# A two-layer attention trunk on one core: exponentials that stay in PSUM, a top-k search by sums of signs, and a new table of segments

## The chip, the cores and the metric

The kernel runs on one core of one Trainium2 chip. The metric is device time in microseconds for one execution of the program. The core has five instruction streams that run side by side and wait for each other through semaphores: TensorE (matmuls and transposes, which write to PSUM; PE in the profile, its weight loads PEld), VectorE (DVE), ScalarE (ACT), GpSimd (POOL) and SyncE (SP), which issues the DMAs. PSUM has eight banks of 512 float32 columns for each of 128 partitions.

## The reference

One sequence of 1024 tokens, 1024 wide, passes two residual layers in float32.

```python
for layer in range(DEPTH):                       # 2
    h = rms_norm(x, ln_g[layer])
    u = h @ w_in                                 # one combined projection
    if layer % 2 == 0:                           # even: A latent attention, B native sparse attention
        y1 = mla_mixer(...) * silu(a_gate)
        y2 = nsa_mixer(...) * silu(b_gate)
    else:                                        # odd: C selected sparse attention, D mLSTM
        y1 = dsa_mixer(...) * silu(c_gate)
        y2 = mlstm_mixer(...) * silu(d_gate)
    y_m = mem_xattn(m_q, mem, ...)
    mix = concatenate([y1, y2, y_m * silu(m_gate)])
    x = x + mix @ w_out[layer]
```

Two pieces matter here. Every attention computes scores, a softmax over them and a product with the values. And the selected sparse attention of the odd layer lets each token attend only to the 256 earlier tokens that an index score ranks highest:

```python
score = einsum('bqh,bqhs->bqs', iw, relu(einsum('bqhd,bsd->bqhs', iq, ik)))
score = where(kpos <= t, score, NEG)
_, sel = lax.top_k(score, 256)
```

## The kernel before

**Who sets the order.** The program is not issued as it is written. Each operation is recorded (class Recorder, line 160) with a cost and with what it depends on; a list scheduler (order, line 302) then places the operations on the five engines and picks the engine where an operation may run on several (flex, line 176: copies go to ACT or DVE, sums and differences to DVE or POOL). Priority comes from the table SEG (line 680): each named piece of work has a start and an end, on which its operations are spread. Tiles come from slots: 8 PSUM banks, 30 pages of 4 KB and 32 of 2 KB in SBUF, and small ones (LIMITS, line 639). Every instruction carries the same source line in the profile, so the profile is read by names of tiles. Five streams result, each in a fixed order: an instruction that waits holds up all behind it on its engine.

**Precision.** Matmuls take fp16. A float32 operand is split in two fp16 halves, hi and lo, and a product takes three matmuls. So each weight and each activation costs a cast (hi) and a subtraction (lo).

**Attention** (attention, line 1277) runs over units of up to 512 columns of scores, or one head where a head has more: for each tile of 128 queries, four heads. One unit passes these steps:

- u_S (1162): matmuls write the scores to PSUM (one bank, or two over 512 columns). DVE takes the negated maximum of each row (nm). In the selected attention, DVE first adds the mask (dmask) and writes the sum to an SBUF page, smask, taking the maximum in the same instruction. Then 11 ln 2 is added to the offset (nm<-nm,lnp, on DVE or POOL), so that the exponentials come out scaled by 2048.
- u_exp (1215): ACT writes exp(score + nm) to an SBUF page P, with the row sums.
- u_split (1224): a part of the units, the turned ones (TURN, line 701: half in latent and native attention, three quarters in selected attention, all in memory attention), are split here: PS is P in two fp16 halves, a cast on ACT or DVE and a subtraction on DVE or POOL.
- u_T (1234): a turned unit is transposed by a DMA, PT<-PS. The other units are transposed by TensorE into PSUM, and ACT copies the high half out (PT); u_lo (1251) subtracts for the low half on DVE.
- u_PV (1257): the product with the values.

With the sizes of this program, 160 units are turned: 104 in the even layer, 56 in the odd one (16 of memory attention, 40 of selected attention, 24 of these 40 with 640 columns or more).

**The top-k search** (topk, line 2049) runs once for query tiles 2 to 4 and once for 5 to 7, on scores of 384 to 1024 columns. It finds the 256th largest score of each row bit by bit: one round for the sign and 31 for the other bits. In each round and for each tile, DVE compares the scores with a candidate and writes ones and zeros (tkj<-score, or tkj<-stop, where stop is the upper half of the scores as bf16, which is enough for the first 15 bits), and ACT sums them (tkj<-tkj, into tkc). Three tiny DVE instructions then set the next candidate (tka, tkd, tkb). After the search DVE builds the mask from comparisons with the threshold and a running count (tkg, tke, tkp, dmask). The search is spread among the projections of the odd layer and the mLSTM.

**v_scale** (line 1107) chooses a power of two for each value tensor and gives its inverse for the result.

Of the kernel before, what the change touches and what calls it, by code (L numbers as in the profile page):

```python
# [8 lines left out]
F = mybir.dt.float32  # L9
R = mybir.dt.float32r  # L10
BF = mybir.dt.bfloat16
H = mybir.dt.float16
I32 = mybir.dt.int32
# [6 lines left out]
NBYTES = {F: 4, R: 4, BF: 2, H: 2, I32: 4}  # L20
# [616 lines left out]
LNP = float(np.float32(11 * np.log(2.0)))  # L637
# [24 lines left out]
def shape_constants():  # L662
# [8 lines left out]
    for i in range(NT):  # L671
# [8 lines left out]
SEG = dict(setup=(-540.765888, -490.733443), norm=(12.964708, 132.050679), e_agate=(31.455813, 704.234339), kv0=(167.224773,  # L680
           345.119047), late=(175.636113, 461.177491), nsak=(275.848244, 1055.795764), q1=(476.701035, 603.438676),
           cmp=(484.672636, 639.334256), nsav=(624.336051, 851.116142), e_kv1=(652.6, 653.6), e_lat=(663.1, 841.289575),
           e_bgate=(688.806149, 749.106149), q0=(713.750502, 956.450502), kv1=(725, 935.4), e_bq=(743.2, 988.9), e_mq=(762.470888,
           932.2), e_kv2=(794.4, 841.5), nsa=(850.7, 1310.2), tab1=(897.605545, 1585.900938), mla0=(911.5, 1001.5), mla1=(952.8,
           1035.2), mem1=(1004.344435, 1330.229828), oA0=(1007.9, 1178.4), mkv0=(1037.7, 1137.062), mem0=(1060.581418, 1262.6),
           oBM0=(1118.8, 1360.2), o_idx=(1297.169979, 1412.178903), topk0=(1312.341201, 1905.3), o_og1=(1334.12618, 1624.221757),
           o_cgate=(1379.576354, 1777.449577), topk1=(1430.809671, 1885.899198), o_og0=(1492.923662, 1808.788497),
           o_mq=(1651.070557, 1759.482667), o_cq=(1677.868104, 1840.650339), o_dqk=(1707.761464, 1804.647378), mlstm=(1753.080505,
           2015.6), o_dv=(1790.7, 1900.9), mkv1=(1795.03316, 1858.78446), oBM1=(1913.5, 2201.9), cv=(1942.975868, 2132.206114),
           dsa=(1984.716978, 2256.916978), oA1=(2154.023358, 2441.25515))  # L690


LOENG = "GV"
# [10 lines left out]
class Trunk:  # L704
# [88 lines left out]
    def setup(self):  # L793
# [9 lines left out]
        self.lnp = self.const([128, 4], F, "lnp")  # L803
        V.memset(self.lnp, LNP)
# [302 lines left out]
    def v_scale(self, views, nh, c=1):  # L1107
# [12 lines left out]
        V.tensor_scalar(e[:, 0, 0:nh], self.spread(m, nh), 1e-30, None, op0=OP.max)  # L1120
        V.tensor_scalar(e[:, 0, 0:nh].bitcast(I32), e[:, 0, 0:nh].bitcast(I32), 0x7F800000, None, op0=OP.bitwise_and)
        V.tensor_scalar(e[:, 1, 0:nh].bitcast(I32), e[:, 0, 0:nh].bitcast(I32), -1.0, float(268 << 23), op0=OP.mult, op1=OP.add)
        V.tensor_scalar(e[:, 2, 0:nh].bitcast(I32), e[:, 0, 0:nh].bitcast(I32), float((14 + c) << 23), None, op0=OP.subtract)
# [38 lines left out]
    def u_S(self, u):  # L1162
# [43 lines left out]
        self.tt(nm, nm, self.lnp[:, 0:per], OP.add, NMENG)  # L1206
# [8 lines left out]
    def u_exp(self, u):  # L1215
        g = u["grp"]
        n, st = u["n"], u["st"]
        p = u["p"] = self.page("P", [128, n * len(u["heads"])])
        for j, h in enumerate(u["heads"]):
            src = self.like(u["sm"][:, j * n:(j + 1) * n], n) if "sm" in u else self.head(u, j)  # L1220
            self.S.activation(self.like(p[:, j * n:(j + 1) * n], n), src, AF.Exp, bias=u["nm"][:, j:j + 1], scale=1.0,
                              accum_out=g["rs"][:, h:h + 1])

    def u_split(self, u):

        if not u["turn"]:
            return
        n = u["n"] * len(u["heads"])
        ps = u["ps"] = self.page("PS", [128, 2, n], H)
        p = u["p"][:, 0:n]  # L1230
        self.copy(ps[:, 0], p)
        self.tt(ps[:, 1], p, ps[:, 0], OP.subtract, LOENG)

    def u_T(self, u):
# [8 lines left out]
        for b0 in range(0, nb, 4):  # L1243
# [4 lines left out]
            self.S.activation(pt[:, 0, b0:b1].rearrange("p k c -> p (k c)"), t[:, 0:128 * (b1 - b0)], AF.Copy)  # L1248
            u["tt"].append((b0, b1, t))

    def u_lo(self, u):
        pt = u["pt"]
        for b0, b1, t in u.get("tt", []):
            f = lambda x: pt[:, x, b0:b1].rearrange("p k c -> p (k c)")
            self.V.tensor_tensor(out=f(1), in0=t[:, 0:128 * (b1 - b0)], in1=f(0), op=OP.subtract)
# [719 lines left out]
    def odd(self, hT, x1tail=None):  # L1975
# [73 lines left out]
        def topk(tiles):  # L2049


            scs = [scores(i, qf) for i, qf in tiles]
            m = len(tiles)
            tops = []
# [4 lines left out]
            cand, base, acc = (self.tiny(m, I32, x) for x in ("tkd", "tkb", "tka"))  # L2059
# [6 lines left out]
            count(0.0, scs)  # L2066
            V.tensor_scalar(base, cnt, 255.5, -1.0, op0=OP.is_lt, op1=OP.mult)
# [398 lines left out]
```

## Time and profile before

| | us |
|---|---|
| median of 3 runs | 1545.11 (1543.31 to 1551.86) |
| the profiled execution | 1550.77 |
| its span, first to last instruction | 1548.9 |
| TensorE busy | 1392.3 |
| DVE busy | 1378.1 |
| ACT busy | 1048.5 |
| POOL busy | 419.7 |
| mean granted TensorE clock | 0.956 |

Busy time is the time in which an engine had at least one instruction running. Rows of groups read: line, engine, operation, output tile <- input tiles, shape and count | busy us, mean ns of one | idle us of the engine before them, and what ended it. A granted clock of 1.00 is full speed.

### The profile page before, as it was taken

To read this page: it belongs to the slowest core of one execution; us is meant where nothing else is said; L and a number is where in the kernel's file an instruction comes from. 1 tells how busy PE (TensorE), PEld (TensorE's weight loads), DVE (VectorE), ACT (ScalarE), POOL (GpSimd) and SP (SyncE) were. 2 spreads that over 40 slices of the span, in tenths; PEclk is the share of its full clock that TensorE was granted. 3 is DMA by queue.
4 is the path that set the end of the run, shared out by engine and by line. 5 is a ranking of instruction groups with operands and counts; after the bars stand their busy time and mean duration, and the time that the engine had idled before them with its cause. 6 is when DMAs were issued, how large, how long until landed. Compare 5 with 4: busy or idle time off the path is not lost.

```text
span 1548.9 us, 30286 instructions
## 1 busy us (share of the span) xinstructions
PE 1392.3 (90%) x10407; PEld 797.4 (51%) x10407; DVE 1378.1 (89%) x3813; ACT 1048.5 (68%) x2498; POOL 419.7 (27%) x527
## 2 busy tenths in 40 slices
PE   4999999978888778969889999999989879998988
PEld 1445546545556655546555554444444455656544
DVE  7765989999999988899889999999999989798994
ACT  7633775576767777786686689999875763466650
POOL 1311244546633242243323200003330212121220
PEclk9999999989999999989999999999998867699999
DMA  9826522367496798979997413201431285299995
GB/s 289 195 75 172 158 71 93 88 150 159 100 179 114 156 183 236 220 138 205 209 235 174 108 48 131 81 25 51 123 109 51 62 181 133 74 207 235 212 232 162
DMA packets 441850, 225.49 MB, mean 146 GB/s; under 512 B 378080, under 2 KB 404320, under 8 KB 441696
## 3 DMA queue, kind: packets, MB, share of 16 engines
q1 hardware_dynamic: 441696, 223.57, 61.0%
q8 instruction: 81, 1.33, 0.4%
q14 instruction: 73, 0.60, 0.1%
HBM read 83.61 MB, written 46.66 MB: 84 GB/s over the span
## 4 chain that ended last, share of the span: by engine, by line
PE 31%; DVE 13%; DMA 4%; issue 2%; ACT 1%; POOL 0%; SPq 0%; ACTq 0%; DVEq 0%
PE psum L558 31%; DMA PT<-PS 3%; DVE tkj L558 1%; DVE nm L558 1%; DVE smask L558 1%; DVE PS L558 1%; DVE wl L558 1%; DVE tkp L558 1%; DVE osp L558 1%; DVE row L558 1%; DVE tke L558 0%; DVE PT L558 0%; DMA oT<-osp 0%; DMA gate<-gate_d 0%; DVE x L558 0%
## 5 line engine op out<-in xcount | busy, mean ns | idle before, releaser
L558 PE MATMUL psum<-wl,hT 128*128 128x512 f16 (+3 forms) x2880 | 669.0, 374 | 11.2 <-DMA hT<-nh 4.0
L558 PEld LDWEIGHTS <-hT 128*128 128x128 f16 x2880 | 280.2, 99 | 315.9 <-issue 36.4
L558 PE MATMUL psum<-wl,oT 128*128 128x512 f16 x960 | 266.3, 382 | 5.7 <-DVE mixM L558 1.9
L558 PEld LDWEIGHTS <-PT 128*128 128x128 f16 x3792 | 223.7, 102 | 92.0 <-DMA PT<-PS 50.7
L558 ACT ACTIVATE P<-psum,nm 128x256 f32<-128x256 f32 (+8 forms) x336 | 191.8, 582 | 90.9 <-POOL nm L558 37.2
L558 POOL TENSOR_TENSOR ms<-ms,nhalf 128x4 f32<-128x4 f32 (+3 forms) x105 | 114.2, 1097 | 430.6 <-DVE ms L558 261.4
L558 PE MATMUL psum<-nv,PT 128*128 128x64 f16 x1584 | 174.8, 195 | 19.6 <-DMA PT<-PS 16.7
L558 DVE TENSOR_REDUCE nm<-psum 128x2 f32<-128x512 f32 (+8 forms) x216 | 162.9, 764 | 16.7 <-PE psum L558 16.4
L558 ACT ACTIVATE tkj<-tkj 128x512 bf16<-128x512 bf16 (+5 forms) x192 | 149.9, 783 | 17.2 <-DVE tkj L558 13.0
L558 PEld LDWEIGHTS <-oT 128*128 128x128 f16 x960 | 93.2, 99 | 102.5 <-issue 6.9
L558 DVE TENSOR_TENSOR PS<-P,PS 128x512 f16<-128x512 f32 (+6 forms) x138 | 116.8, 849 | 1.3 <-ACT PS L558 1.2
L558 PE MATMUL psum<-cst,P 128*128 128x128 f32 x502 | 102.8, 292 | 13.2 <-ACT P L558 9.1
L558 PEld LDWEIGHTS <-qf 128*128 128x128 f16 x832 | 77.6, 103 | 49.3 <-issue 15.2
L558 ACT ACTIVATE wj<-wr 128x1024 bf16<-128x1024 f32 (+4 forms) x76 | 77.7, 1024 | 27.8 <-DMA wr<-w_out 16.7
L558 ACT ACTIVATE PT<-psum 128x512 f16<-128x512 f32 (+3 forms) x160 | 76.5, 504 | 29.3 <-PE psum L558 21.7
L558 PE MATMUL psum<-nkst,qf 128*128 128x320 f16 (+5 forms) x384 | 90.2, 319 | 5.8 <-DVE PT L558 2.5
L558 DVE TENSOR_TENSOR wl<-wr,wl 128x1024 f16<-128x1024 f32 (+3 forms) x79 | 93.7, 1190 | 1.8 <-ACT wl L558 1.6
L558 DVE TENSOR_TENSOR PT<-psum,PT 128x512 f16<-128x512 f32 (+3 forms) x160 | 88.1, 566 | 2.0 <-ACT PT L558 1.7
L558 PE MATMUL psum<-cvp,PT 128*128 128x64 f16 x864 | 70.9, 195 | 13.1 <-DMA PT<-PS 10.1
L558 PEld LDWEIGHTS psum<-cst,P 128*128 128x128 f32 x502 | 65.7, 142 | 32.0 <-ACT P L558 13.6
L558 PE MATMUL psum<-vp,PT 128*128 128x64 f16 x864 | 65.3, 197 | 11.9 <-DMA PT<-PS 6.7
L558 POOL TENSOR_TENSOR nm<-nm,lnp 128x1 f32<-128x1 f32 (+2 forms) x116 | 30.6, 265 | 149.1 <-DVE nm L558 133.2
(494 smaller groups left out, 2894.0 us busy)
## 6 DMA issues: line engine op xcount, KB each, us to landing
wr<-even_w_in SPq DMA_DIRECT2D x20, 512.0 KB, 6.0
wr<-w_out SPq DMA_DIRECT2D x20, 512.0 KB, 5.1
wr<-odd_w_in SPq DMA_DIRECT2D x20, 512.0 KB, 4.9
gate<-gate_d SPq DMA_DIRECT2D x32, 256.0 KB, 3.8
gate_d<-gu SPq DMA_DIRECT2D x24, 256.0 KB, 2.2
qa_d<-mqT SPq DMA_DIRECT2D x16, 384.0 KB, 2.4
xt<-x SPq DMA_DIRECT2D x8, 512.0 KB, 10.3
x<-x SPq DMA_DIRECT2D x8, 512.0 KB, 4.7
```

The costliest lines, as they stand in the source:

```text
L558: r = getattr(engines[o.eng], meth)(*[res(a) for a in args], **{k: res(v) for k, v in kw.items()})
```

## The change

It has three parts and a new table.

1. **The split.** The offset 11 ln 2 goes; exponentials are no longer scaled. In a turned unit ACT writes the exponential over the scores, in PSUM. The cast multiplies by 2048, and the subtraction is one DVE instruction that computes 2048 x - hi (sub with a scale, line 769: scalar_tensor_tensor, on DVE only). The masked scores of the selected attention also stay in PSUM. Units that aren't turned still write P to SBUF; their factor of 2048 moves to the copy out of the transpose's PSUM tile. v_scale's inverse has 11 more in its exponent, since the row sums have lost the 2048.

2. **The search.** In each round ACT computes the sign of (threshold - score), or with the other sign, and sums it; one DVE instruction compares the sum with a limit. For the lower 16 bits the scores are replaced once, for each tile, by a page tkr: the lower half of a score where its upper half equals the threshold found, a large number where it is above, zero where it is below. No comparison on DVE is left in the rounds.

3. **The table** SEG has other numbers.

```diff
-SEG = dict(setup=(-540.765888, -490.733443), norm=(12.964708, 132.050679), e_agate=(31.455813, 704.234339), kv0=(167.224773,
...
+SEG = dict(setup=(-1576.69593, -601.132494), mem1=(-688.598351, 20.410205), e_agate=(30.600801, 726.724683), norm=(40.663363,
...
     def u_S(self, u):
...
         if g.get("addmask") is not None:
-            sm = u["sm"] = self.page("smask")
             for j in range(per):
-                V.tensor_tensor_reduce(out=self.like(sm[:, j * n:(j + 1) * n], n), in0=self.head(u, j),
-                                       in1=self.like(g["addmask"], n), scale=1.0,
+                V.tensor_tensor_reduce(out=self.head(u, j), in0=self.head(u, j), in1=self.like(g["addmask"], n), scale=1.0,
                                        scalar=-3e38, op0=OP.add, op1=OP.max, accum_out=nm[:, j:j + 1])
-            V.tensor_scalar(nm, nm, -1.0, LNP, op0=OP.mult, op1=OP.add)
-            return
+            V.tensor_scalar(nm, nm, -1.0, None, op0=OP.mult)
...
-        self.tt(nm, nm, self.lnp[:, 0:per], OP.add, NMENG)
...
     def u_exp(self, u):
         g = u["grp"]
-        n, st = u["n"], u["st"]
-        p = u["p"] = self.page("P", [128, n * len(u["heads"])])
+        n = u["n"]
+        if not u["turn"]:
+            u["p"] = self.page("P", [128, n * len(u["heads"])])
         for j, h in enumerate(u["heads"]):
-            src = self.like(u["sm"][:, j * n:(j + 1) * n], n) if "sm" in u else self.head(u, j)
-            self.S.activation(self.like(p[:, j * n:(j + 1) * n], n), src, AF.Exp, bias=u["nm"][:, j:j + 1], scale=1.0,
-                              accum_out=g["rs"][:, h:h + 1])
+            src = self.head(u, j)
+            dst = src if u["turn"] else self.like(u["p"][:, j * n:(j + 1) * n], n)
+            self.S.activation(dst, src, AF.Exp, bias=u["nm"][:, j:j + 1], scale=1.0, accum_out=g["rs"][:, h:h + 1])
     def u_split(self, u):
...
-        p = u["p"][:, 0:n]
-        self.copy(ps[:, 0], p)
-        self.tt(ps[:, 1], p, ps[:, 0], OP.subtract, LOENG)
+        self.copy(f(0), src, scale=PSCALE)
+        self.sub(f(1), src, f(0), scale=PSCALE)
...
         def topk(tiles):
...
-            def count(thr, data):
-                for j, sc in enumerate(data):
-                    junk = self.page("tkj", sc.shape, BF)
-                    V.tensor_scalar(junk, sc, thr if isinstance(thr, float) else thr[:, j:j + 1], None, op0=OP.is_ge)
-                    S.activation(junk, junk, AF.Copy, accum_out=cnt[:, j:j + 1])
...
-            for bit in range(30, -1, -1):
-                count(cand.bitcast(F), tops if bit >= 16 else scs)
-                V.tensor_scalar(acc, cnt, 255.5, float(1 << bit), op0=OP.is_gt, op1=OP.mult)
-                if bit:
-                    V.scalar_tensor_tensor(out=cand, in0=acc, scalar=1 << (bit - 1), in1=base, op0=OP.bitwise_xor, op1=OP.bitwise_xor)
-                V.tensor_tensor(out=base, in0=base, in1=acc, op=OP.bitwise_xor)
...
+            def search(data, bits, up, level, side):
+                V.tensor_scalar(nxt, base, up(bits[0]), None, op0=OP.bitwise_xor)
+                for x, bit in enumerate(bits):
+                    t = level(nxt if x == 0 else thr)
+                    for j, d in enumerate(data):
+                        junk = self.page("tkj", d.shape, BF)
+                        S.activation(junk, d, AF.Sign, bias=t[:, j:j + 1], scale=side if side == -1.0 else side[:, j:j + 1], accum_out=cnt[:, j:j + 1])
+                    if x + 1 < len(bits):
+                        V.tensor_scalar(nxt, base, up(bits[x + 1]), None, op0=OP.bitwise_xor)
+                    V.scalar_tensor_tensor(out=acc, in0=cnt, scalar=1.0, in1=lim, op0=OP.mult, op1=OP.is_lt)
+                    if x + 1 < len(bits):
+                        V.scalar_tensor_tensor(out=thr, in0=acc, scalar=bit, in1=nxt, op0=OP.logical_shift_left, op1=OP.bitwise_xor)
+                    V.scalar_tensor_tensor(out=base, in0=acc, scalar=bit, in1=base, op0=OP.logical_shift_left, op1=OP.bitwise_xor)
...
+            search(tops, list(range(30, 15, -1)), lambda b: (1 << b) - (1 << 15), lambda t: t.bitcast(F), isg)
...
+                V.tensor_scalar(eq, tops[j], c(sig), c(top), op0=OP.mult, op1=OP.is_equal)
+                V.tensor_scalar(ab, tops[j], c(sig), c(top), op0=OP.mult, op1=OP.is_gt)
+                r = self.page("tkr", sc.shape)
+                V.scalar_tensor_tensor(out=r, in0=sc.bitcast(U16)[:, 0::2], scalar=1.0, in1=eq, op0=OP.add, op1=OP.mult)
+                V.scalar_tensor_tensor(out=r, in0=ab, scalar=131072.0, in1=r, op0=OP.mult, op1=OP.add)
...
+            search(low, list(range(15, -1, -1)), lambda b: 1 << b, half, -1.0)
```

**In the streams: DVE, lower bits of the search, before.** tkj is the comparison of a tile's scores, tkd the candidate, tka and tkb the round's result; 384, 512 and 640 columns belong to the first search, 768, 896 and 1024 to the second. wl and wr are weights, the rest belongs to the projections.

```order
L558 SCALAR_TENSOR_TENSOR tkd_13821<-tka_13879,tkb_13815 128x3
L558 SCALAR_TENSOR_TENSOR gu_14738<-gth_14761,gu_14738 128x256
L558 TENSOR_TENSOR tkb_13815<-tkb_13815,tka_13879 128x3
L558 CAST wl_14802<-wr_13902 128x1024
L558 TENSOR_SCALAR tkj_14808<-score_13222,tkd_13821 128x768
L558 TENSOR_SCALAR tkj_14815<-score_12765,tkd_13430 128x512
L558 TENSOR_TENSOR wl_14802<-wr_13902,wl_14802 128x1024
L558 TENSOR_SCALAR tkj_14829<-score_13350,tkd_13821 128x896
```

The same engine after, also in the lower bits: tkn is the next candidate before the round's result, tkv the threshold plus a half; row belongs to the mLSTM.

```order
L559 SCALAR_TENSOR_TENSOR tka_13605<-tkc_13098,tkl_102 128x3
L559 COPY mp_112<-row_3335_15341 4x7
L559 TENSOR_TENSOR qsq_15058<-qu_15056,tab_11926 128x512
L559 SCALAR_TENSOR_TENSOR tkd_13608<-tka_13605,tkn_114 128x3
L559 SCALAR_TENSOR_TENSOR tkb_110<-tka_13605,tkb_110 128x3
L559 SCALAR_TENSOR_TENSOR ogu_15309<-ogt_15287,ogu_15309 128x256
L559 TENSOR_SCALAR tkv_14590<-tkd_13608 128x3
```

The wide comparisons have left DVE's stream; four or five instructions on three columns stand in their place in each round.

**ACT, selected attention at 896 columns, before.** P is the exponential, rs its row sums, PS its high half, PT a transposed unit's.

```order
L558 ACTIVATE P_19144,rs_19129<-smask_19109,nm_19110 128x896
L558 ACTIVATE PT_19164<-psum 128x384
L558 ACTIVATE PT_19164<-psum 128x512
L558 ACTIVATE P_19180,rs_19129<-smask_19148,nm_19149 128x896
L558 ACTIVATE osp_19206<-mixA_18488,oe_19160 128x512
L558 ACTIVATE PS_19210<-P_19180 128x896
```

After, at the same size:

```order
L559 ACTIVATE P_18695,rs_18696<-psum,nm_18671 128x896
L559 ACTIVATE psum,rs_18696<-psum,nm_18680 128x2x448
L559 ACTIVATE psum,rs_18696<-psum,nm_18703 128x2x448
L559 ACTIVATE PT_18738<-psum 128x512
L559 ACTIVATE PT_18738<-psum 128x384
L559 ACTIVATE PS_18751<-psum 128x896
```

The exponential of a turned unit goes back to its two PSUM banks and the high half is read from there; in both, one ACT instruction or more stands between the exponential and its copy.

**DVE, selected attention at 896 columns, before.** smask is the masked score, the ISA row with dmask masks and takes the maximum.

```order
L558 CAST PS_19184<-P_19144 128x896
L558 TENSOR_TENSOR PT_19164<-psum,PT_19164 128x512
L558 TENSOR_TENSOR PS_19184<-P_19144,PS_19184 128x896
L558 ISA smask_19217,nm_19218<-psum,dmask_17154 128x896
L558 ISA nm_19218 128x1
L558 TENSOR_TENSOR PS_19210<-P_19180,PS_19210 128x896
```

After:

```order
L559 TENSOR_TENSOR mixA_18122<-psum,cf_18614 128x256
L559 SCALAR_TENSOR_TENSOR x_3933_18145<-psum,oe_18296,x_3933_18145 128x512
L559 SCALAR_TENSOR_TENSOR PS_18751<-psum,PS_18751 128x896
L559 ISA psum,nm_18820<-psum,dmask_16692 128x2x448
L559 ISA nm_18820 128x1
```

The subtraction that ends a unit's split now also ends that unit's hold on its banks.

**Counts in the order.** The search's 186 comparisons on DVE go. Of the 160 subtractions of the split, 138 stood on DVE and 22 on POOL; all 160 stand on DVE. Of its 160 copies, 93 stood on DVE and 67 on ACT; 59 and 101 now. The 216 additions of the offset (100 on DVE, 82 of these ahead of the odd layer, and 116 on POOL) go. TensorE has 19434 instructions in both. ACT loads its function tables 7 times instead of 5.

More of the change, by code (lines that the diff above doesn't have):

```diff
@@ L636 @@
 NT = 8
[L637 removed]
+PSCALE = 2048.0
 SPLIT = 3
@@ L1227, in u_split @@
             return
-        n = u["n"] * len(u["heads"])
-        ps = u["ps"] = self.page("PS", [128, 2, n], H)
-        p = u["p"][:, 0:n]
-        self.copy(ps[:, 0], p)
-        self.tt(ps[:, 1], p, ps[:, 0], OP.subtract, LOENG)
+        n, per = u["n"], len(u["heads"])
+        ps = u["ps"] = self.page("PS", [128, 2, n * per], H)
+        k = min(per, max(1, 512 // u["st"]))
+        if n > 512 or per == 1:
+            src, f = self.head(u, 0), lambda x: self.like(ps[:, x], n)
+        else:
+            src = u["s"][:, :, 0:k * u["st"]].rearrange("p b (h c) -> p b h c", h=k)[:, :, :, 0:n]
+            f = lambda x: ps[:, x].rearrange("p (b h c) -> p b h c", b=per // k, h=k)
+        self.copy(f(0), src, scale=PSCALE)
+        self.sub(f(1), src, f(0), scale=PSCALE)
     def u_T(self, u):
@@ L2053, in topk @@
             m = len(tiles)
+            ns = [sc.shape[1] for sc in scs]
             tops = []
@@ new lines, in topk @@
+            for j, n in enumerate(ns):
+                V.memset(lim[:, j:j + 1], n - 511.0)
+            acc, base, nxt, thr = (self.tiny(m, I32, x) for x in ("tka", "tkb", "tkn", "tkd"))
+            def search(data, bits, up, level, side):
[11 more added lines that the diff above has]
+                    V.scalar_tensor_tensor(out=base, in0=acc, scalar=bit, in1=base, op0=OP.logical_shift_left, op1=OP.bitwise_xor)
@@ new lines, in topk @@
+            for j, sc in enumerate(scs):
+                junk = self.page("tkj", sc.shape, BF)
+                V.tensor_scalar(junk, sc, 0.0, None, op0=OP.is_ge)
+                S.activation(junk, junk, AF.Copy, accum_out=cnt[:, j:j + 1])
+            sig, isg = self.tiny(m, F, "tks"), self.tiny(m, F, "tkf")
+            V.tensor_scalar(sig, cnt, 255.5, 2.0, op0=OP.is_gt, op1=OP.mult)
+            V.tensor_scalar(isg, sig, -1.0, 1.0, op0=OP.mult, op1=OP.add)
+            V.tensor_scalar(sig, sig, -1.0, None, op0=OP.add)
@@ new lines, in topk @@
+            V.tensor_tensor(out=lim, in0=lim, in1=sig, op=OP.mult)
+            V.memset(base, 0)
+            search(tops, list(range(30, 15, -1)), lambda b: (1 << b) - (1 << 15), lambda t: t.bitcast(F), isg)
+            top = self.tiny(m, F, "tkt")
+            V.tensor_copy(top, base.bitcast(F))
+            low = []
+            for j, sc in enumerate(scs):
+                eq = self.page("tkq", sc.shape, BF)
+                ab = self.page("tkh", sc.shape, BF)
+                c = lambda x: x[:, j:j + 1]
+                V.tensor_scalar(eq, tops[j], c(sig), c(top), op0=OP.mult, op1=OP.is_equal)
[3 more added lines that the diff above has]
+                V.scalar_tensor_tensor(out=r, in0=ab, scalar=131072.0, in1=r, op0=OP.mult, op1=OP.add)
+                low.append(r)
+                scs[j] = None
@@ L2075, in topk, with half @@
+            del tops, sc
+            V.memset(base, 0)
+            lev = self.tiny(m, F, "tkv")
+            def half(t):
+                V.tensor_scalar(lev, t, 0.5, None, op0=OP.add)
+                return lev
+            search(low, list(range(15, -1, -1)), lambda b: 1 << b, half, -1.0)
+            V.tensor_scalar(lev, base, 1.0, None, op0=OP.add)
             for j, (i, _) in enumerate(tiles):
-                sc = scs[j]
+                r = low[j]
                 n = 128 * (i + 1)
-                thr = base[:, j:j + 1].bitcast(F)
+                t = lev[:, j:j + 1]
@@ L2090, in topk @@
                 V.tensor_scalar(masks[i], gt, 1.0, 1e30, op0=OP.subtract, op1=OP.mult)
+                low[j] = None
         def post_dv(i, ps, wi):
```

44 lines of the change are left out of this document (21 added, 23 removed).

## The prediction

> **What bounds the kernel now.** I read the page first, then the same time cut into six stages, then the chain of waits.
>
> ```profile
> span 1548.9 us, 30286 instructions
> PE 1392.3 (90%) x10407; PEld 797.4 (51%) x10407; DVE 1378.1 (89%) x3813; ACT 1048.5 (68%) x2498; POOL 419.7 (27%) x527
> ```
>
> TensorE and VectorE (DVE) are equally full over the whole span, so an average says nothing. The next view has one row for each stage: start and end, then busy us (and count) of each engine, then the granted TensorE clock.
>
> ```profile
> core 0: us, PE busy (x) PEld busy (x) DVE busy (x) ACT busy (x) POOL busy (x), PEclk, DMA share, GB/s
> 0.00:300.00 300.00, 274.64 (x1402) 140.58 (x1403) 234.31 (x839) 174.29 (x367) 90.25 (x109) 1.00 0.52 145
> 300.00:850.00 550.00, 464.86 (x5036) 309.79 (x5034) 512.16 (x1248) 398.19 (x1039) 210.15 (x306) 0.97 0.82 173
> 850.00:1150.00 300.00, 298.54 (x1467) 145.39 (x1465) 288.48 (x822) 261.01 (x581) 53.08 (x49) 1.00 0.27 84
> 1150.00:1350.00 200.00, 175.21 (x872) 97.56 (x870) 178.61 (x452) 115.23 (x286) 33.46 (x32) 0.76 0.41 103
> 1350.00:1450.00 100.00, 93.45 (x872) 57.62 (x871) 90.55 (x285) 59.89 (x150) 15.60 (x20) 0.98 0.99 213
> 1450.00:1549.00 99.00, 85.62 (x769) 46.48 (x766) 74.00 (x173) 39.95 (x80) 17.11 (x13) 0.98 0.84 201
> ```
>
> I call them A to F. A is projections of the even layer, C those of the odd layer: TensorE leaves 1.5 of 300 us free in C. B is attention of the even layer: DVE is busy 512 of 550 us, TensorE idles 85. D holds mLSTM and the end of the top-k search: TensorE idles 24.8 of 200 us and has a clock of 0.76. E and F are sparse attention and the end. The chain that ended last agrees (start, length, what held it):
>
> ```profile
> 928.44 188.09 PE psum L558 x882
> ...
> 1131.21 2.12 DVE tkj L558 x4
> ...
> 1207.85 1.12 DVE tkj L558 x2
> ...
> 1229.95 1.13 DVE tkj L558 x2
> ...
> 1486.14 1.13 DVE smask L558
> ```
>
> Through C it is matmuls alone; through D it hops between DVE instructions, the comparisons of the search (tkj) among them; in E and F it passes the masking of scores (smask). So work taken off DVE pays in D, partly in B, E and F, and not in C unless it lets D's work come forward.
>
> **Part by part: the top-k search.**
>
> ```profile
> L558 DVE TENSOR_SCALAR tkj<-score,tkd 128x768 bf16<-128x768 f32 (+5 forms) x96 | 57.6, 619 | 0.0
> L558 DVE TENSOR_SCALAR tkj<-stop,tkd 128x512 bf16<-128x512 bf16 (+5 forms) x90 | 32.7, 395 | 0.0
> L558 DVE SCALAR_TENSOR_TENSOR tkd<-tka,tkb 128x3 int32<-128x3 int32 x60 | 9.5, 160 | 0.1
> L558 DVE SCALAR_TENSOR_TENSOR score<-relu,iw,score 128x1024 f32<-128x1024 f32 x7 | 9.0, 1280 | 0.0
> ```
>
> The comparisons go: 96 x 619 ns + 90 x 395 ns = 57.6 + 32.7 = 90.3 us less on DVE. DVE gains tiny instructions: one more per bit in each of two searches (62), a half added to each low-bit threshold (32) and some 16 of set-up, 110 x 160 ns = 18 us. Building the low-half values needs, per tile, two comparisons of bf16 (12 x 0.40 = 5 us), two two-operand passes (1280 ns at 1024 columns; the mean tile has 704, so 12 x 0.88 = 11 us) and one subtraction (6 x 0.62 = 4 us). Sum: 90 - 38 = 52 us off DVE. Where those 90 us stand is the next answer, that tile's instructions alone (stage, DVE busy, ACT busy):
>
> ```profile
> 850.00:1150.00 300.00, 73.77 (x158) 128.84 (x314) 1.00 0.27 84
> 1150.00:1350.00 200.00, 19.53 (x35) 29.98 (x70) 0.76 0.41 103
> ```
>
> Four fifths lie in C, under matmuls that fill it. On ACT the number of counts stays 192; 186 of them get a per-partition operand or two. The nearest rows without and with one, both 512 columns out of PSUM:
>
> ```profile
> L558 ACT ACTIVATE xqf<-psum 128x512 fp32r<-128x512 f32 x11 | 6.3, 603 | 0.8 <-PE psum L558 0.8
> L558 ACT ACTIVATE gth<-psum,winv 128x512 f32<-128x512 f32 x24 | 16.3, 681 | 11.4 <-PE psum L558 11.1 <-POOL lms L558 0.3
> ```
>
> That is 78 ns, so 186 x 78 = 15 us, and 22 us if the second operand of the 90 top-half counts costs as much again; no row shows two.
>
> **The split in PSUM.** (PS is the pair of fp16 halves, P the exponential.)
>
> ```profile
> L558 DVE TENSOR_TENSOR PS<-P,PS 128x512 f16<-128x512 f32 (+6 forms) x138 | 116.8, 849 | 1.3 <-ACT PS L558 1.2
> L558 DVE CAST PS<-P 128x512 f16<-128x512 f32 (+6 forms) x93 | 48.1, 517 | 6.2 <-ACT P L558 2.4 <-DMA PT<-PS 1.7 <-PE psum L558 0.7
> L558 ACT ACTIVATE PS<-P 128x512 f16<-128x512 f32 (+5 forms) x67 | 45.5, 678 | 1.0 <-ACT oj L558 0.2
> L558 POOL TENSOR_TENSOR PS<-P,PS 128x512 f16<-128x512 f32 (+5 forms) x22 | 31.8, 1446 | 66.8 <-ACT PS L558 27.3 <-DVE nm L558 16.6 <-DVE PS L558 9.8
> L558 DVE TENSOR_TENSOR PT<-psum,PT 128x512 f16<-128x512 f32 x92 | 62.0, 682 | 1.4 <-ACT PT L558 1.3
> L558 DVE CUSTOM_DVE_ANT_0 smask<-psum,dmask 128x1024 f32<-128x1024 f32 x8 | 9.7, 1216 | 0.2 <-PE psum L558 0.2
> L558 DVE TENSOR_SCALAR gu<-psum,winv 128x512 f32<-128x512 f32 x8 | 6.0, 744 | 0.0
> ```
>
> All 160 subtractions become DVE's. PSUM rows give 682 ns at 512 columns and 1216 at 1024, a line of 148 + 1.043 n. Over the order's shapes (8 of 256, 18 of 384, 62 of 512, 30 of 640, 14 each of 768, 896 and 1024) that is 125 us; 59 copies stay on DVE at the same line, 48 us (52 with the 744 row, which has a pointer). DVE: 173 for 165, 8 us more. POOL loses 31.8. ACT takes 101 copies for 67, 34 x 678 ns = +23 us. The exponential written to PSUM has no row; its length could move by what a DVE write does, so I bound it by +-78 ns (the step between the two rows above) and take zero: 192 x 78 ns is 15 us of ACT, which has 152 idle us in B.
>
> **The offset.**
>
> ```profile
> L558 POOL TENSOR_TENSOR nm<-nm,lnp 128x1 f32<-128x1 f32 (+2 forms) x116 | 30.6, 265 | 149.1 <-DVE nm L558 133.2 <-DVE cf L558 8.2 <-DVE ms L558 7.4
> L558 DVE TENSOR_TENSOR nm<-nm,lnp 128x1 f32<-128x1 f32 (+2 forms) x100 | 17.7, 177 | 0.2
> ```
>
> All 216 go: 17.7 us of DVE, 30.6 of POOL, and one hop between the maximum and the exponential. 82 of the 100 stand before the odd layer in DVE's order, so 14.5 us leave B.
>
> **The rest.** Two more table loads appear, because the sine and the cosine now stand apart on ACT; both lie in A's first 50 us, under matmuls; bare they would be 2.6 us by this row:
>
> ```profile
> L558 ACT ACT_TABLE_LOAD x5 | 6.4, 1283 | 0.8 <-PEq L2452 0.7
> ```
>
> The rescheduling leaves each engine's sequence of stages as it was; TensorE has the same 19434 rows.
>
> **The sum.** DVE: -52 - 17.7 + 8 = -62 us; POOL -62; ACT +38 to +45. On the path: A and C give 0. B: 14.5 us less, and 8 x 104/160 = 5 more for its 104 of the 160 subtractions, is 9 us off DVE; I take 5 of it, since part of TensorE's idle there has other causes. D: the 52 us come off C and D together, where DVE was busy 467 of 500 us; D can shrink until TensorE has no gap, 24.8 us; I take 18. E and F: 3 us of offsets go and 7 subtractions come back from POOL, while 17 copies go to ACT; 1 us. Together 24 us. The profiled execution took 1550.77 us (span plus 1.9), so 1526.8 by it; it lies 5.7 us over the median of the three runs, 1545.11, and against that median the forecast is 1521.
>
> D's clock is weighed apart. TensorE is busy 10 of 10 us in two neighbouring stretches and the clock stays at half:
>
> ```profile
> 1310.00:1320.00 10.00, 10.00 (x31) 6.54 (x32) 9.74 (x39) 6.64 (x15) 1.35 (x1) 0.50 0.12 23
> 1320.00:1330.00 10.00, 10.00 (x37) 6.78 (x37) 7.24 (x16) 6.28 (x12) 2.12 (x1) 0.50 0.00 0
> ```
>
> So I credit no clock to fewer gaps. The Trainium skill, "TensorE: Matmul & The Clock Gate", Part 1, says that half clock is the idle state and that about 3.4 us of sustained activity lifts it; by it, D without gaps would also run at full clock. The rows above, 20 us without a gap, don't bear that out.
>
> **Rivals.**
> (1) Full clock in D. If a denser stream does lift it, D's 175.2 busy us at 0.76 become 133, 42 us less: 1521 - 42 = 1479; half of it gives 1500. For it: the clock is 1.00 in C, which is dense. Against it: the two rows above. This is where the skill's rule would lead. 8%.
>
> (2) The relief is hidden. Without DVE's comparisons the search hangs on ACT alone, and in C that engine is full:
>
> ```profile
> 950.00:1000.00 50.00, 50.00 (x234) 23.14 (x233) 48.59 (x155) 48.80 (x116) 0.00 (x0) 1.00 0.47 156
> ```
>
> 48.8 of 50, and 15 to 22 us come on top. If that delays masks and evacuations by about what DVE frees in D (18), 5 or 6 us are left: 1540. Against it: DVE can take evacuations over, and has 52 us to do so. 15%.
>
> (3) PSUM runs out: the slower side. Before, a masked score left its two banks after smask, and another turned unit after the exponential; now both hold them until the subtraction. At 1024 columns that adds this exponential, a copy and a subtraction:
>
> ```profile
> L558 ACT ACTIVATE P<-smask,nm 128x1024 f32<-128x1024 f32 x8 | 9.2, 1145 | 8.9 <-DVE nm L558 8.5 <-DVE oe L558 0.3
> ```
>
> 1.15 + 0.68 + 1.22 = 3.0 us for the 24 turned units of 640 columns or more in E and F, and 0.68 + 0.69 = 1.4 us for the 104 in B: 72 + 146 = 218 us of added hold, in eight banks. All of it is covered if another bank is free for the next scores. From 11% uncovered on (24 of 218) the gain is gone; at a quarter, 54 us, the time is 1521 + 54 = 1575. For it: TensorE already idles 85 us in B. Against it: units up to 512 columns take one bank. The Trainium skill's "PSUM — Partial Sum Buffer", its summary of rules, says to evacuate promptly because the space is tight; no row here shows a wait for a bank as such. 12%.
>
> **How the numbers follow.** The forecast's case (10 to 45 us gained) has 65%, the rivals 8, 15 and 12. About 0.5%, 7.7 us, is what a measurement of this kernel can tell from no change. Faster: 65 + 8 + 2 of rival 2 = 75%. Same: the other 13. Slower: 12. The range goes down to 1498 (B's 9, D's 24.8 and 13 us of clock, 47 in all) and up to 1550, past rival 2 with an exponential dearer by 15 us partly uncovered; most of (3) and the far half of (1) stay out, under 20%.
>
> **What would show it.** Right: DVE busy near 1316, POOL near 357, ACT near 1090; no tkj on DVE, none of PS on POOL; TensorE's idle time in the mLSTM stage under 10 us and the stage near 180; C as long as before. Wrong: TensorE's idle time in B above 85 us with waits for scores' tiles (3); ACT over 49 of 50 us through the search with TensorE gaps beside it (2); a clock over 0.9 in D (1).

## The result, and the profile after

The changed kernel takes **1524.25 us** (median of 4 runs, 1516.0 to 1524.7), the kernel before, on the same chip, 1545.78 us (median of 4, 1543.31 to 1551.86): a ratio of 0.984, 95% interval 0.981 to 0.987. The forecast was 1521. Its profiled execution took 1524.7 us.

The page's head:

```profile
span 1522.9 us, 29899 instructions
PE 1397.5 (92%) x10407; PEld 796.4 (52%) x10407; DVE 1355.0 (89%) x3681; ACT 1061.1 (70%) x2460; POOL 380.2 (25%) x436
```

DVE lost 23.1 us, POOL 39.5; ACT gained 12.6. Both TensorE and DVE are as full as before, in a shorter span. Where it became shorter is told by one landmark: the matmuls of the index scores (tile cist), with which the odd layer's attention work begins. Of before, then of after (duration min/median/max, first and last start):

```profile
L558 PE MATMUL psum<-cist,xqf x80: 304/495/586, 859.4 to 961.0; 128*128 128x384 f32 x24, 128*128 128x512 f32 x24, 128*128 128x320 f32 x16, 128*128 128x448 f32 x16
```

```profile
L559 PE MATMUL psum<-cist,xqf x80: 303/534/882, 834.6 to 944.4; 128*128 128x384 f32 x24, 128*128 128x512 f32 x24, 128*128 128x320 f32 x16, 128*128 128x448 f32 x16
```

The first starts at 834.6 us instead of 859.4: 24.8 of the span's 26.0 us are gained by then, ahead of the search. From there to the end it took 1548.9 - 859.4 = 689.5 us and takes 1522.9 - 834.6 = 688.3. I call these two lengths the front and the rear. The stages of after, with borders moved along (start and end, then busy us and count of PE, PEld, DVE, ACT, POOL, then the clock):

```profile
300.00:825.00 525.00, 464.91 (x5013) 309.50 (x5012) 495.85 (x1101) 399.28 (x1034) 175.62 (x220) 0.95 0.81 179
825.00:1125.00 300.00, 291.87 (x1425) 140.14 (x1424) 266.31 (x765) 259.81 (x533) 35.15 (x42) 0.99 0.28 83
1125.00:1323.00 198.00, 178.75 (x1056) 101.05 (x1055) 180.96 (x519) 124.02 (x324) 44.27 (x46) 0.89 0.43 109
1323.00:1523.00 200.00, 184.69 (x1506) 104.17 (x1504) 163.59 (x404) 103.17 (x212) 24.46 (x24) 0.92 0.83 206
950.00:1000.00 50.00, 48.85 (x230) 22.52 (x229) 33.22 (x118) 49.58 (x101) 0.00 (x0) 1.00 0.12 40
```

B: the same 465 us of TensorE's work in 525 us instead of 550, idle time 60 instead of 85. C: DVE's load fell, by 22 us, but TensorE now idles 8 us there, where it idled 1.5. D: DVE has 181 of 198 us, as much as before (178.6 of 200); TensorE idles 19.3 us there instead of 24.8, where the forecast had a stage near 180 us with under 10. The last row is a stretch of the search: ACT 49.6 of 50 us, DVE a third idle. What TensorE waited for in B, before:

```profile
PE psum L558 <- DMA PT<-PS: 28.4, 19, 5.0
PE psum L558 <- ACT P L558: 19.4, 26, 2.2
PE psum L558 <- DVE PT L558: 16.0, 22, 1.7
PE psum L558 <- DVE vdg L558: 7.2, 1, 7.2
```

And after (us in total, times, longest):

```profile
PE psum L559 <- DVE PS L559: 17.3, 18, 2.3
PE psum L559 <- DMA PT<-PS: 12.2, 15, 1.9
PE psum L559 <- ACT P L559: 7.2, 6, 2.6
PE psum L559 <- DVE PT L559: 6.0, 8, 1.6
PE psum L559 <- DVE vdg L559: 3.2, 2, 1.7
```

Waits for transposing DMAs, exponentials and low halves are each less than half; new is a wait for PS, the subtraction that now releases a unit's banks (17.3 us): the forecast's third rival in small. ACT's own waits for the row maxima in B did not get shorter, 55.6 us before and 54.3 after, though the offset between maximum and exponential is gone:

```profile
ACT P L558 <- POOL nm L558: 32.3, 28, 3.2
ACT P L558 <- DVE nm L558: 23.3, 18, 3.2
```

```profile
ACT P L559 <- DVE nm L559: 34.7, 33, 3.8
ACT psum L559 <- DVE nm L559: 19.6, 21, 3.1
```

### The profile page after: what moved, and what is told of

Read it like the earlier page. It is cut to its first block, busy times and chain, and to the rows that moved or that the text cites. A ratio compares the mean times of both kernels' runs of the same rounds, so it can differ in the third digit from the quotient of the medians.

```text
span 1522.9 us, 29899 instructions
## 1 busy us (share of the span) xinstructions
PE 1397.5 (92%) x10407; PEld 796.4 (52%) x10407; DVE 1355.0 (89%) x3681; ACT 1061.1 (70%) x2460; POOL 380.2 (25%) x436
## 5 line engine op out<-in xcount | busy, mean ns | idle before, releaser
L559 PEld LDWEIGHTS <-PT 128*128 128x128 f16 x3792 | 248.4, 103 | 66.4 <-DMA PT<-PS 27.1
L559 ACT ACTIVATE psum<-psum,nm 128x256 f32<-128x256 f32 (+8 forms) x234 | 137.4, 591 | 68.1 <-DVE nm L559 53.4
L559 ACT ACTIVATE P<-psum,nm 128x64 f32<-128x64 f32 (+8 forms) x150 | 92.4, 623 | 57.7 <-DVE nm L559 46.0
L559 DVE SCALAR_TENSOR_TENSOR PS<-psum,PS 128x512 f16<-128x512 f32 (+6 forms) x160 | 124.1, 783 | 2.5 <-ACT PS L559 2.4
L559 PEld LDWEIGHTS <-qf 128*128 128x128 f16 x832 | 78.6, 103 | 66.4 <-issue 23.1
L559 PE MATMUL psum<-cvp,PT 128*128 128x64 f16 x864 | 106.1, 200 | 5.6 <-DMA PT<-PS 5.6
L559 DVE TENSOR_TENSOR wl<-wr,wl 128x1024 f16<-128x1024 f32 (+4 forms) x76 | 92.8, 1230 | 0.8 <-ACT wl L559 0.5
L559 ACT ACTIVATE tkj<-tkr,tkv 128x384 bf16<-128x384 f32 (+5 forms) x96 | 83.8, 879 | 13.5 <-DVE tkv L559 7.5
L559 DVE SCALAR_TENSOR_TENSOR PT<-psum,PT 128x512 f16<-128x512 f32 (+3 forms) x160 | 88.2, 566 | 5.3 <-ACT PT L559 5.2
L559 ACT ACTIVATE wj<-wr 128x1024 bf16<-128x1024 f32 (+6 forms) x73 | 74.1, 1020 | 13.7 <-DMA wr<-even_w_in 7.7
L559 ACT ACTIVATE tkj<-stop,tkd,tkf 128x768 bf16<-128x768 bf16 (+5 forms) x84 | 80.8, 970 | 0.4 <-DVE tkb L559 0.4
```

Source lines behind the costliest of these rows:

```text
L559: r = getattr(engines[o.eng], meth)(*[res(a) for a in args], **{k: res(v) for k, v in kw.items()})
```

## The theories

**Theory 1** is the forecast's: the search's relief of DVE moves the end, in C and D (18 us), the split and the offset give little (5). Its rival, from the forecast: the relief is hidden, because the search then hangs on ACT. **Theory 2**: the split and the offset give it, in B. **Theory 3**: the new table gives it by itself. **Theory 4**, formed after the first runs: the time hangs on how well a table's order fits the work that it holds, so an edit shows its worth only with an order made for it.

Two kinds of kernels were made. Some are scheduled anew, so that an edit changes all five streams. Others keep a kernel's finished order and have instructions left out, put in or replaced as they are issued, so that the order of all others stays.

## Experiments: parts, scheduled anew

**The new table on the kernel before.** Only SEG's numbers are replaced:

```diff
-SEG = dict(setup=(-540.765888, -490.733443), norm=(12.964708, 132.050679), e_agate=(31.455813, 704.234339), kv0=(167.224773,
...
+SEG = dict(setup=(-1576.69593, -601.132494), mem1=(-688.598351, 20.410205), e_agate=(30.600801, 726.724683), norm=(40.663363,
...
```

> The kernel before with the new table of segments and nothing else. Theory 1 (the forecast's: the search's relief of DVE gives most, in C and D) and theory 2 (the split and the offset give it, in B) both expect no gain: 1546 us, within 8 us, since the new segments were laid out for other instructions. Theory 3 (the table itself gives the gain) expects 1524 to 1530 us and the first score matmul of the index near 835 us instead of 859.

Measured: 1581.74 us, ratio to before 1.024 (1.021 to 1.027). Theory 3 falls, and so does what theories 1 and 2 took for granted, that the table is neutral: it costs 36 us.

**The old table on the changed kernel**, the same replacement the other way round.

> The changed kernel with the old table of segments. Theories 1 and 2 expect most of the gain to stay: 1522 to 1534 us. Theory 3 (the table gives the gain) expects 1546 us or more.

Measured: 1556.36 us, ratio 1.008 (1.005 to 1.011): slower than before. Theories 1 and 2 miss; theory 3's figure is met, but theory 3 had fallen with the run above.

**The search alone**, with the new table: topk as in the change, u_S, u_exp, u_split as before.

```diff
-                    V.tensor_scalar(junk, sc, thr if isinstance(thr, float) else thr[:, j:j + 1], None, op0=OP.is_ge)
-                    S.activation(junk, junk, AF.Copy, accum_out=cnt[:, j:j + 1])
+                        S.activation(junk, d, AF.Sign, bias=t[:, j:j + 1], scale=side if side == -1.0 else side[:, j:j + 1], accum_out=cnt[:, j:j + 1])
```

> New table and new search; the split, the offset and the masked scores as before. Theory 1 expects 18 of the 25 us: 1528 us, DVE near 1325 us busy, the index's first score matmul near 859 us as before and the gain behind it. Theory 2 expects 1540 to 1550 us: B as long as before, and nothing gained behind it, since ACT is full through the search. Theory 3 expects the time of the table alone.

Measured: 1574.11 us, ratio 1.020 (1.017 to 1.023): 7.6 us under the table alone. All three figures are missed; theory 3's, the time of the table alone, is the nearest.

**The split alone**, with the new table: u_S, u_exp, u_split as in the change, topk as before.

```diff
-        self.copy(ps[:, 0], p)
-        self.tt(ps[:, 1], p, ps[:, 0], OP.subtract, LOENG)
+        self.copy(f(0), src, scale=PSCALE)
+        self.sub(f(1), src, f(0), scale=PSCALE)
```

> New table, split in PSUM and no offset; the search as before. Theory 1 expects 5 to 6 us: 1540 us. Theory 2 expects 1520 to 1528 us, with the index's first score matmul near 835 us instead of 859. Theory 3 expects the time of the table alone.

Measured: 1538.62 us, ratio 0.996 (0.995 to 0.998). Theory 1's figure is met, theory 2's missed by 10 us. But its index scores begin at 830.6 us, so theory 2's landmark came true, and the rear is 15 us longer than before. With the new search beside it, on the same table, this is the changed kernel: 14.4 us less, and the rear 16 us shorter.

**The split alone, with the old table**, the same edit beside before's SEG.

> Old table, split in PSUM and no offset, the search as before. Theory 1 expects 1540 us (5 us from the split), theory 2 expects 1520 to 1525 us. With the changed kernel on the old table at 1556 us, theory 4 (an order is worth what its table was laid out for) expects no gain here, 1545 to 1560 us, and the new search then worth little on the old table.

Measured: 1558.92 us, ratio 1.009 (1.006 to 1.012), as theory 4 had it. And the new search on the old table (1556.36 against 1558.92) is worth 3 us, which the two intervals don't tell from none.

**The control: one entry of the table nudged.**

```diff
-           988.9), e_mq=(765.062608, 934.79172), e_kv2=(784.700952, 841.5), nsa=(850.7, 1310.2), mla0=(911.5, 1001.5),
+           988.9), e_mq=(765.062608, 934.79172), e_kv2=(784.700952, 841.5), nsa=(850.7, 1310.2), mla0=(914.5, 1004.5),
```

> The changed kernel with one entry of its table, the start and end of the first half of latent attention, three units later; the same work, scheduled anew. If the scheduler's orders are alike for tables that are nearly alike, the time stays at 1524 us within 3 us, and differences of 10 us between kernels scheduled anew can be put down to their edits. If an order is worth tens of us by itself, it comes out 10 us or more away (slower, since the table was laid out for this kernel), and every comparison of kernels scheduled anew carries that much uncertainty.

Measured: 1560.72 us, ratio to before 1.011 (1.007 to 1.014), 36 us over the changed kernel with the very same work. Its landmark and what TensorE waited for from 300 to 870 us:

```profile
L559 PE MATMUL psum<-cist,xqf x80: 305/524/585, 857.7 to 967.5; 128*128 128x384 f32 x24, 128*128 128x512 f32 x24, 128*128 128x320 f32 x16, 128*128 128x448 f32 x16
```

```profile
PE psum L559 <- DVE PS L559: 20.4, 23, 1.8
PE psum L559 <- DVE PT L559: 16.5, 19, 1.9
PE psum L559 <- DMA PT<-PS: 16.3, 15, 3.5
PE psum L559 <- ACT P L559: 10.0, 11, 2.2
```

The same operations, though the scheduler also chose some engines anew (3707 instructions on DVE for 3681), and 857.7 us instead of 834.6: nearly the whole front gain is gone, in waits of the same kinds, those for low halves above all (PT on DVE, 16.5 us for 6.0). This control rules the reading of all runs of this kind: a difference between two kernels scheduled anew says nothing of an edit when it is not well over the difference that an order makes.

**The hop, known to the scheduler.**

```diff
             V.tensor_reduce(out=nm, in_=s[:, :, 0:n], axis=AX.X, op=OP.max, negate=True)
+        if g.get("addmask") is None:
+            self.tt(nm, nm, self.ones[:, 0:per], OP.mult, "GV")
```

> The changed kernel with the small instruction between maximum and exponential back (nm times one, on DVE or POOL), this time known to the scheduler, which makes its order with it. Theory 1 (5 us, DVE's load): 1529 us. Theory 2 (the hop in stage B, 22 us when put into the finished order): 1540 to 1550 us, the index's first score matmul 15 us later or more. Theory 4 (what counts is that the order was made for the work it holds): the scheduler hides most of the hop again, 1535 us or less.

Measured: 1566.04 us, ratio 1.015 (1.010 to 1.020). All three figures are missed, theory 2's by least. The scheduler did not hide the hop, against theory 4; but the nudge alone costs 36 of these 42 us.

**Turned units split from SBUF, without the offset.**

```diff
-        if not u["turn"]:
+        if True:
...
-            dst = src if u["turn"] else self.like(u["p"][:, j * n:(j + 1) * n], n)
+            dst = self.like(u["p"][:, j * n:(j + 1) * n], n)
...
+        src, f = u["p"][:, 0:n * per], lambda x: ps[:, x]
         self.copy(f(0), src, scale=PSCALE)
```

> The changed kernel, but turned units write their exponential to an SBUF page and are split from there, as before, with the factor 2048 in cast and subtraction and without the offset. Scheduled anew. If the gain in B comes from staying in PSUM, it is lost here: 1545 us, the index's first score matmul near 860 us. If it comes from the offset's end, it stays: 1524 to 1532 us. Rival 3 of the forecast (PSUM runs out) expects it faster than the changed kernel: under 1518 us.

Measured: 1566.26 us, ratio 1.015 (1.011 to 1.018). All three figures are missed, though the landmark, 861.3 us, is that of a gain from staying in PSUM. The time is 42 us from the changed kernel, little further than an order is (36), so neither this nor the run above tells the offset from the stay in PSUM. That PSUM's shortage costs the changed kernel much is not borne out.

All runs of this kind together; front and rear are of the profiled execution, span split at the first index score. That execution lies up to 8 us off the median (nudge 8 under it, the split with the old table 6 over it):

| | work | table | us | front | rear |
|---|---|---|---|---|---|
| before | old | its own | 1545.78 | 859.4 | 689.5 |
| after | new | its own | 1524.25 | 834.6 | 688.3 |
| split alone | split new | after's | 1538.62 | 830.6 | 704.4 |
| table alone | old | after's | 1581.74 | 875.8 | 704.8 |
| search alone | search new | after's | 1574.11 | 873.8 | 697.4 |
| split alone, old table | split new | before's | 1558.92 | 864.9 | 698.6 |
| old table | new | before's | 1556.36 | 860.2 | 692.0 |
| nudge | new | after's, nudged | 1560.72 | 857.7 | 692.9 |
| hop planned | new, hop | after's | 1566.04 | 863.6 | 696.9 |
| P in SBUF | new, P in SBUF | after's | 1566.26 | 861.3 | 704.8 |

Both kernels' own tables beat the other orders of the same work by 32 to 36 us (1581.74 against 1545.78; 1556.36 and 1560.72 against 1524.25). With its own table each, the change gives 21.5 us; with a table not its own each, 1581.74 against 1556.36 or 1560.72, 21 to 25; on one table for both it loses 11 us (the old one) or gains 57 (the new one). The front goes with the split: 873.8 and 875.8 without it, 857.7 to 864.9 with it, in orders not laid out for their work; 859.4 and 834.6 (830.6) in those that were. For the rear and the search these runs tell nothing firm: 698.6 to 704.8 with the old search, 692.0 to 697.4 with the new one (P in SBUF, 704.8, apart), a gap smaller than the distance of a profiled execution from its median, and no more than 1.2 us between the two tuned kernels. These are few orders, and two orders of one work can lie 36 us apart: this suggests where the gain is from, and does not show it.

## Experiments: parts, the order kept

**Comparisons taken out of the kernel before.** As instructions are issued, the comparison is passed over, and the sum that follows reads the scores:

```diff
+            if kw.get("op0") == OP.is_ge and args[0].t.name.startswith("tkj_") and isinstance(args[2], View):
+                uses[args[1].t] = uses.get(args[1].t, 0) + 1
+                if uses[args[1].t] < (15 if args[1].dtype == BF else 16):
+                    thr[args[0].t] = args
+                    continue
+            if args and isinstance(args[0], View) and args[0].t in thr and args[1].t is args[0].t:
+                junk, sc, t = thr.pop(args[0].t)[:3]
...
+                args, kw = (junk, sc, AF.Sign), dict(bias=t, scale=side, accum_out=kw["accum_out"])
...
```

> The kernel before, every instruction in its place, but 174 of the 186 comparisons of the search on DVE left out, and ACT summing signs straight from the scores against the candidate, one operand for the float32 scores and two for the bf16 ones; the round's test has one limit for three tiles, so the threshold found is not the 256th score. Nothing is rescheduled, so the time tells what DVE's relief alone is worth. Theory 1 (the relief moves the end, through C and D) expects DVE near 1293 us busy, TensorE's idle time in D down from 24.8 to under 10 us, and 1528 us. The rival (the relief is hidden, the search then hangs on ACT) expects 1540 us or more.

Measured: 1547.03 us, ratio 1.001 (0.999 to 1.004). The relief, together with its price on ACT (1067.3 us busy for 1048.5, since sums of signs take longer), is worth nothing in the old order: theory 1 falls here, its rival stands. DVE's busy time fell by 61.5 us to 1316.6, less than expected. Its C and D:

```profile
850.00:1150.00 300.00, 292.09 (x1417) 141.05 (x1416) 229.97 (x668) 271.86 (x564) 46.42 (x47) 0.99 0.25 78
1150.00:1350.00 200.00, 178.51 (x910) 98.72 (x907) 170.40 (x425) 122.20 (x298) 35.58 (x34) 0.80 0.43 111
```

DVE has 70 idle us in C instead of 11.5, and TensorE does 6 us less there; in D its idle time goes from 24.8 to 21.5. DVE's longest wait from 850 to 1350 us, and the chain of waits from 1008 us, show why:

```profile
DVE tka L572 <- ACT tkj L572: 35.8, 39, 2.5
```

```profile
1012.67 3.18 ACT tkj L572 x7
...
1017.46 4.76 ACT tkj L572 x10
...
1029.77 3.20 ACT tkj L572 x7
...
1041.74 3.99 ACT tkj L572 x9
```

In before the chain ran through matmuls here (from 928 to 1117 us). Now it hangs, up to 1061 us, on ACT's sums, between which ACT still casts weights (wj, wr) and evacuates. The last sum of the search starts at 1251.9 us, in before at 1247.9.

**The offset taken out of the kernel before.**

```diff
+            if kw.get("in1") is not None and kw["in1"].t.name.startswith("lnp_"):
+                continue
```

> The kernel before, every instruction in its place, but the 216 additions of the offset (100 on DVE, 116 on POOL) left out, so that exponentials of unmasked units are not scaled by 2048. Theory 1 (5 us, by DVE's load alone) expects 1540 us. Theory 2 (the hop itself, DVE to POOL to ACT, is what stage B waits for: ACT waited 32 us there for POOL's nm) expects 1525 to 1530 us, with the index's first score matmul 15 to 20 us earlier.

Measured: 1541.33 us, ratio 0.999 (0.996 to 1.001): at most 6 us, perhaps none. Theory 1's figure is met, theory 2's missed, and the index scores begin at 860.4 us, no earlier. What ACT, then TensorE, waited for in B:

```profile
ACT P L560 <- DVE nm L560: 46.0, 35, 3.5
ACT PT L560 <- PE psum L560: 25.5, 28, 3.6
```

```profile
PE psum L560 <- DMA PT<-PS: 30.8, 24, 4.0
PE psum L560 <- DVE PT L560: 18.4, 22, 3.6
PE psum L560 <- ACT P L560: 10.4, 16, 1.4
```

ACT's wait for maxima fell from 55.6 to 46.0 us and TensorE's for exponentials from 19.4 to 10.4; TensorE's waits for DMA and low halves rose from 28.4 and 16.0 to 30.8 and 18.4: in part what comes next in the fixed streams takes the wait over.

**Comparisons put back into the changed kernel.**

```diff
+            if len(args) > 2 and args[2] == AF.Sign and "accum_out" in kw:
+                engines["V"].tensor_scalar(res(args[0]), res(args[1]), res(kw["bias"]), None, op0=OP.is_ge)
```

> The changed kernel, every instruction in its place, with a comparison of the same size and tile put back on DVE ahead of each of the 186 sums of signs, which then wait for it. Theory 1 expects some 18 us back: 1542 us. The rival (hidden) expects under 1530 us.

Measured: 1609.03 us, ratio 1.040 (1.036 to 1.044), 85 us over the changed kernel; both expectations were far off. These two rows of comparisons are 91.7 us:

```profile
L560 DVE TENSOR_SCALAR tkj<-tkr,tkv 128x384 bf16<-128x384 f32 (+5 forms) x96 | 57.6, 607 | 1.1 <-ACT tkj L561 1.1
L560 DVE TENSOR_SCALAR tkj<-stop,tkd 128x768 bf16<-128x768 bf16 (+5 forms) x84 | 34.1, 420 | 0.0
```

```profile
ACT tkj L561 <- DVE tkj L560: 75.4, 84, 6.5
```

ACT waits 75 us for them, with evacuations behind it. DVE's busy time rises by 75.0 us, to 1430.0, and the time by more. The index scores begin at 834.7 us, so all of it is lost behind the front. The edit puts on DVE a load and before each sum a wait, and no run tells the two apart. About the same comparisons that are worth nothing when taken from an order laid out around them (174 of them) cost 85 us when put into an order laid out without them (186).

**The hop put back into the changed kernel.**

```diff
...
+            if kw.get("negate"):
+                nm = View(kw["out"].t, kw["out"].ops[:1], None, F).real()
+                hops += 1
+                one = self.ones[:, 0:nm.shape[1]].real()
+                engines["VG"[hops % 2]].tensor_tensor(out=nm, in0=nm, in1=one, op=OP.mult)
```

> The changed kernel, every instruction in its place, with a small instruction (nm times one, on DVE and POOL by turns) put back behind each maximum of an unmasked unit, ahead of its exponential. Theory 1 expects 5 us: 1529 us. Theory 2 (the hop is what stage B waited for) expects 1540 us or more, with TensorE's idle time of the first 825 us up by 15 us.

Measured: 1549.78 us, ratio 1.003 (1.001 to 1.005), 25.5 us over the changed kernel. Theory 2's figure is met. The loss lies in the front; the lines below are of the profiled execution, the fastest of ten (1542.93), the waits from 300 to 835 us:

```profile
L560 PE MATMUL psum<-cist,xqf x80: 303/534/827, 856.6 to 966.5; 128*128 128x384 f32 x24, 128*128 128x512 f32 x24, 128*128 128x320 f32 x16, 128*128 128x448 f32 x16
```

```profile
ACT P L560 <- POOL nm L565: 37.3, 37, 3.9
...
ACT P L560 <- DVE nm L565: 14.0, 10, 2.8
ACT psum L560 <- POOL nm L565: 13.2, 15, 3.0
```

The index scores begin at 856.6 us, 22.0 later, and the rear is 684.5. TensorE's idle time in the first 825 us is 99.1 us instead of 82.8, and ACT's waits for maxima (with 11.4 us of psum on DVE's nm) are 75.9 instead of 54.3. So the changed kernel's front stands on the absence of these instructions; without a new order that absence is worth 0 to 6 us. No run put as many small instructions elsewhere, so the hop's delay is not told from its load on DVE and POOL.

## Why the forecast came out right, point by point

- **The time** (1521, measured 1524) was right, and so was the sign. **The sum behind it was not**: it had 5 us in B, 18 in D and 1 in E and F. Measured are 24.8 in the front and 1.2 in the rear. Terms that were wrong by some 20 us each way cancelled, so the number came right by luck.
- **The step that failed first**: "D can shrink until TensorE has no gap, 24.8 us; I take 18." It took a lower sum on DVE for a shorter D. DVE's load fell in C, where TensorE was full (288.5 to 266.3 us), and not in D (178.6 to 181.0). In before's order with the comparisons left out, DVE's load in D was 8 us lower, and TensorE's gaps there were still 21.5. After, the chain of waits still hops between DVE instructions in D, the search's final masks and the mLSTM's:

```profile
1256.52 0.52 DVE tkr L559
1257.04 2.09 DVE tkp L559
1259.18 0.60 DVE dss L559
1259.86 0.71 DVE tkg L559 x2
```

- **The second**: "The rescheduling leaves each engine's sequence of stages as it was", with which the order was given no price. One entry of the table, moved by three, is worth 36 us here, more than the whole forecast gain.
- **B, "I take 5 of it"**, counted DVE's load only. In the changed kernel's order the hop alone is worth 22 us of the front. In before's order the 5 was about right (4 us, not told from none), though the 14.5 us of additions behind it took only 4.0 us off DVE's busy time in B (512.2 to 508.2).
- **Rival 2** (hidden, ACT full) is what happens in before's order: with the comparisons left out ACT is busy all of the 100 us from 950 us on, and TensorE idles 4.7 us beside it, where it idled none. In the changed kernel ACT is as full in one stretch only (49.6 of 50 us, then 47.2), and whether the relief is hidden there is not shown: on the new table the search gave 8 us without the split and 14 with it, less than an order is worth. The rival's 1540 held B at 5. **Rival 3** (PSUM) came as 17.3 us of waits for PS, within a stage that got 25 us shorter. **Rival 1** (full clock): D's clock rose from 0.76 to 0.89, but the last stage's fell from 0.98 to 0.92, and over the whole span it is 0.957 for 0.956. TensorE stays at half clock in stretches that the profile, which models the ends of matmuls, shows as busy without a gap, as before:

```profile
1310.00:1320.00 10.00, 10.00 (x43) 6.39 (x42) 5.98 (x23) 4.16 (x13) 1.37 (x2) 0.50 0.18 40
1320.00:1330.00 10.00, 10.00 (x48) 6.81 (x48) 6.00 (x22) 3.93 (x10) 0.96 (x1) 0.50 0.95 197
```

- **Prices** held where a row had the same shape: the subtraction from PSUM

```profile
L559 DVE SCALAR_TENSOR_TENSOR PS<-psum,PS 128x512 f16<-128x512 f32 (+6 forms) x160 | 124.1, 783 | 2.5 <-ACT PS L559 2.4
L559 DVE TENSOR_SCALAR PS<-psum 128x512 f16<-128x512 f32 (+6 forms) x59 | 47.3, 806 | 1.7 <-ACT psum L559 1.5
```

  124 us for 125, the copies 47 for 48. The bound on exponentials into PSUM took 192 of them; there are 234, so it was 18 us, not 15, and zero was about right. The sums of engines did not hold: DVE 1355 for 1316, ACT 1061 for 1090, POOL 380 for 357. One reason is the scheduler, which chooses the engine of most copies and many differences and gave DVE's free time other work (gu<-psum,winv, 13 on DVE before, 16 after, among them). The other is that the forecast added up lengths of instructions, which overlap in the traces. The 174 comparisons left out of before were 84.8 us long together, and DVE's busy time fell by 61.5; the 100 additions of the offset were 17.7 us, and it fell by 6.5 (1378.1 to 1371.6).

**What stays open**: how the front's 25 us divide between the offset, the stay in PSUM and the order. The offset's part holds only in the order made without it; the stay in PSUM could not be tried in a kept order, since a bank's next user is placed by its release. Open too is what the search gives in the changed kernel's order: the run that puts the comparisons back tells it only together with the wait that they add.

## What to carry to other kernels

Where a scheduler lays out in-order streams, price the order as a term of its own: nudge one number of its table and see how far the time moves, before a difference between two schedules is put down to an edit. Removing work from a finished order, or adding it, tells what that order hangs on, and the two need not be alike: here nothing one way and 85 us the other. And ask of a relieved engine in which stage its load falls, not by how much in all, and count busy time, not lengths of instructions: here 85 us of lengths were 61.5 us of busy time.

## What the runs showed of the hardware

In these sums an operand for each partition costs ACT some 95 ns. The sums of signs after, over the same sizes as before's 783 ns without any (the row below, x192):

```profile
L558 ACT ACTIVATE tkj<-tkj 128x512 bf16<-128x512 bf16 (+5 forms) x192 | 149.9, 783 | 17.2 <-DVE tkj L558 13.0 <-DVE vsc L558 1.1 <-DVE ms L558 0.9
```

```profile
L559 ACT ACTIVATE tkj<-tkr,tkv 128x384 bf16<-128x384 f32 (+5 forms) x96 | 83.8, 879 | 13.5 <-DVE tkv L559 7.5 <-DVE dss L559 5.7
L559 ACT ACTIVATE tkj<-stop,tkd,tkf 128x768 bf16<-128x768 bf16 (+5 forms) x84 | 80.8, 970 | 0.4 <-DVE tkb L559 0.4
```

One operand gives 879 - 783 = 96 ns, which also holds the step from a copy to a sign and from bf16 to float32; two give 970 - 783 = 187. The forecast had 78 and left the second open. The Trainium skill, "ScalarE: Activation LUTs", What ACT_TABLE_LOAD costs, says that each such pointer operand adds about 93 ns; the trace agrees, for the second as for the first.

An exponential written over its scores in PSUM costs no more than one to SBUF of the same size. It takes 660 against 686 ns at 512 columns and 291 against 332 at 64; at 256 columns the two are alike:

```profile
L559 ACT ACTIVATE psum<-psum,nm 128x256 f32<-128x256 f32 x82 | 37.6, 469 | 9.2 <-DVE nm L559 8.8
...
L559 ACT ACTIVATE P<-psum,nm 128x256 f32<-128x256 f32 x14 | 6.5, 472 | 3.1 <-DVE nm L559 2.8 <-PE psum L559 0.2
```
